# Weight buffers 68 bytes longer, and four raw buffers instead of five, in a one-core transformer layer

## The chip, the core and the metric

The kernel runs on one core of a Trainium2 chip. The core has a matrix engine (TensorE, written PE in the profile; its weight loads are PEld), a vector engine (VectorE, DVE), a scalar engine (ScalarE, ACT), a general engine (GpSimd, POOL) and a sequencer that mostly issues transfers (SyncE, SP). They run their own instruction streams in order and wait for one another by semaphores. Operands lie in an on-chip memory of 128 partitions (SBUF); matrix results go to a second one (PSUM) of eight banks. Transfers between SBUF and the large off-chip memory are carried out by 16 DMA engines.

The metric is the device time of one execution in microseconds (us), lower is better.

## The reference

One decoder layer on 256 tokens of width 2048, all in float32:

- `h = rmsnorm(x)`, then one projection `h @ w_in` into q, k, v of eight attention heads (A) and the low-rank latents of eight more (B);
- A: causal attention in three dilated windows, merged by their softmax denominators; B: latent attention, whose q, k and v come from the latents through `w_uq` and `w_ukv`;
- `x = x + rmsnorm(concat(A, B) @ w_out)`;
- `x = x + rmsnorm(relu(rmsnorm(x) @ w_up)**2 @ w_down)`, where `w_up` is 2048 x 8192 and `w_down` 8192 x 2048.

Nearly all of the arithmetic is in the five matrix products with the large weights; the two of the feed-forward part alone are 134 MB.

## The kernel before

**Split products.** A float32 product is computed as three products of a shorter format. Each operand is split into a part `hi`, rounded to that format, and the rest `lo`; then `a @ w` is `a_hi @ w_hi + a_hi @ w_lo + a_lo @ w_hi`. Each of the three is one matmul on PE with a 128 x 128 block of activations as the operand that is loaded first (PEld) and 512 columns of the weights as the one that streams through (function `three`, and `proj` in the attention part; the helper `mm` is line 296, so nearly every matmul has that line).

**The weight stream.** Class `Weights` takes the weights in the order in which PE will use them, in tiles of 128 partitions x 1024 columns (512 KB). For each tile `emit` does the following, and this is the code that the change touches:

1. `load` takes the next buffer with the tag `raw` and issues the transfer on SP (line 190). There are `RAW_BUFS` such buffers, used in turn; the transfer has to wait until the tile that used the buffer last has been read by its last reader, a subtraction on DVE.
2. ACT rounds `raw` into a buffer `hi` (line 306, or 310 where a gain is multiplied in).
3. DVE subtracts, `lo = raw - hi` (line 307, or 311 with the gain). After that the raw buffer is free.

There are `W_BUFS = 8` buffers for `hi` and as many for `lo`; they come free when PE has used the tile. `emit` runs `W_AHEAD = 6` tiles ahead of the one that PE is about to use. The small pieces of `x` transposed that the first projection needs go through the same raw buffers (`x_load`, line 527).

**Made tiles.** A part of the feed-forward products is computed with seven block products in place of eight (function `seven_products`). For these, DVE first adds blocks of weights that POOL loads in 1 MB pieces (`ab`, `ab_down`, `c` and others, line 374; in the last groups of `w_up` two raw buffers instead), and the sums are split like weights.

**Order.** The whole program order is written by the Python code, which keeps a clock of its own (class `Flow`): chains such as the softmax of a head or the evacuation of an accumulator are started with a delay, and their instructions are put between the matmuls when that clock passes. So every engine's order is fixed; on ACT and DVE the splits of weights that are still far ahead stand in one row with the evacuations that PE waits for soon. An up-projection's evacuation is: `r = relu(acc)` on ACT (line 937), four transposes on PE (`rt`, line 300), a square on ACT (line 949).

**Where the tiles lie.** The left side of SBUF holds first small constants, then the pool `wp` with raw, `hi` and `lo` buffers, then what the current part needs; activations are on the right. In the built program every raw, `hi` and `lo` buffer is 4096 bytes per partition long, and all of them begin at an address that is 480 modulo 512 (the first `hi` at 38880). The same holds for nearly every activation block that PE loads for a split product, which is 128 columns, or 512 bytes, of a tile that begins at 480 modulo 512. Small padding tiles such as `con_pad` and `pa_pad` see to that.

Of the kernel before, what the change touches and what calls it, by code (L numbers as in the profile page):

```python
# [19 lines left out]
F32R = mybir.dt.float32r  # L20
# [6 lines left out]
P = 128  # L27
# [18 lines left out]
CW = 1024  # L46
# [24 lines left out]

RAW_BUFS, W_BUFS, W_AHEAD, AHEAD_NORM = 5, 8, 6, 4

APART = (5, 7)

# [91 lines left out]
class Weights:  # L169
# [23 lines left out]
    def emit(self, upto):  # L193
        upto = min(upto, self.done.index(False) + self.limit, len(self.specs))
        while len(self.tiles) < upto:
            i = len(self.tiles)
            spec = self.specs[i]
            make = len(spec) == 1
            for f in self.first.pop(i, ()):
                f()  # L200
            if not make:
                src, nk, n, g = (*spec, None)[:4]
                w = nk * n
                raw = self.load(src if len(src.shape) == 3 else src.rearrange("(k p) n -> p k n", p=P), w, f"raw{i}")
                for f in self.after.pop(i, ()):
                    f()
            hi = self.pool.tile([P, CW], F32R, tag="hi", bufs=self.bufs, name=f"hi{i}")
            lo = self.pool.tile([P, CW], F32R, tag="lo", bufs=self.bufs, name=f"lo{i}")
            if make:
                spec[0](hi, lo)  # L210
                self.tiles.append((hi, lo))
                continue

            def v(t):
                return t[:, :w].rearrange("p (k n) -> p k n", k=nk)

            cuts = [(o, min(o + 512, w)) for o in range(0, w, 512)] if i < FINE else [(0, w)]
            for o, e in cuts:
                self.split_fn(hi[:, o:e], lo[:, o:e], raw[:, o:e], g)
            self.tiles.append((v(hi), v(lo)))  # L220
# [1088 lines left out]
```

## Time and profile before

| | |
|---|---|
| median of 2 runs | 1047.33 us (1047.23 to 1047.43) |
| profiled execution, first to last instruction (span) | 1045.7 us |
| PE busy in it | 1035.7 us, 99% |
| DVE busy | 838.7 us, 80% |
| ACT busy | 630.4 us, 60% |
| POOL busy | 51.5 us, 5% |
| bytes moved by DMA | 229.33 MB, mean 219 GB/s |

The profile gives one span for the execution and no other time of its own; the runs' median is 1.6 us above it, which is what lies around the first and the last instruction together with the difference from one execution to the next. A busy PE need not be PE at its best pace, since the end of a matmul is modelled; the distance from one matmul's start to the next is the better measure. In the tables of waits, "A <- B" means that engine A stood idle until B's instruction had ended. A row such as "x4 ... 4.62" is four instructions in a row, which took 4.62 us together.

### The profile page before, as it was taken

How to read it: one execution, taken by the hardware profiler on the slowest of the kernel's cores; microseconds unless marked ns; L12 is line 12 of the kernel's file. 1: busy time of each engine (PE TensorE's matmuls, PEld its weight loads, DVE VectorE, ACT ScalarE, POOL GpSimd, SP SyncE). 2: the span in 40 equal slices, each digit the busy share in tenths (PEclk: the TensorE clock that was granted, in tenths of full speed). 3: DMA queues.
4: the chain of work that ended last, by engine and by line, in shares of the span. 5: the costliest groups of instructions: out<-in, count | busy, mean ns of one | idle time of the engine just before them, and what ended most of it. 6: DMA issues, size and time to landing. Idle time of an engine off the chain costs nothing.

```text
span 1045.7 us, 13378 instructions
## 1 busy us (share of the span) xinstructions
PE 1035.7 (99%) x4837; PEld 863.2 (83%) x4837; DVE 838.7 (80%) x1122; ACT 630.4 (60%) x848; POOL 51.5 (5%) x83
## 2 busy tenths in 40 slices
PE   9999999999999999999999999999999999999996
PEld 6888889888888888888888888888888888888885
DVE  6676536567557669999999999897899978999995
ACT  6674436565545566665765667666567564766661
POOL 0000000000000000000000000000000000111100
PEclk9999999999999999999999999999999999999998
DMA  9975547454447295646657356378778767698952
GB/s 303 370 229 148 140 129 241 146 162 153 150 156 236 92 360 188 216 147 207 202 185 246 121 201 207 113 253 325 274 276 303 265 232 261 238 332 323 356 204 83
DMA packets 79938, 229.33 MB, mean 219 GB/s; under 512 B 6912, under 2 KB 11520, under 8 KB 79488
## 3 DMA queue, kind: packets, MB, share of 16 engines
q1 hardware_dynamic: 64576, 171.47, 48.9%
q0 software_dynamic: 14864, 56.63, 15.2%
q8 instruction: 38, 0.62, 0.3%
q10 hardware_dynamic: 432, 0.37, 0.1%
q14 instruction: 28, 0.23, 0.1%
HBM read 212.72 MB, written 15.73 MB: 218 GB/s over the span
## 4 chain that ended last, share of the span: by engine, by line
PE 97%; DVE 1%; issue 1%; ACT 0%; POOL 0%; DVEq 0%; POOLq 0%; ACTq 0%
PE y L296 25%; PE acc_u L296 24%; PE acc_o L296 8%; PE m L296 7%; PE md L296 5%; PE acc_qk L296 4%; PE acc_v L296 4%; PE acc_ckv L296 2%; PE acc_ukv L296 2%; PE acc_q L296 2%; PE acc_cq L296 2%; PE acc_k L296 2%; PE acc_uq L296 2%; PE rt L300 1%; PE sc_b L296 1%
## 5 line engine op out<-in xcount | busy, mean ns | idle before, releaser
L307 DVE TENSOR_TENSOR lo<-raw,hi 128x1024 fp32r<-128x1024 f32 (+3 forms) x213 | 241.5, 1152 | 89.8 <-ACT hi L306 89.1
L306 ACT ACTIVATE hi<-raw 128x1024 fp32r<-128x1024 f32 (+3 forms) x213 | 209.9, 999 | 73.6 <-PE y L296 16.1
L296 PE MATMUL y<-hi,uhi 128*128 128x512 f32 x370 | 144.4, 390 | 0.0
L296 PE MATMUL y<-hi,ulo 128*128 128x512 f32 x370 | 144.1, 389 | 0.0
L296 PE MATMUL y<-lo,uhi 128*128 128x512 f32 x370 | 144.0, 389 | 0.0
L296 PE MATMUL acc_u<-hi,hT_hi 128*128 128x512 f32 x356 | 141.7, 398 | 0.0
L296 PE MATMUL acc_u<-hi,hT_lo 128*128 128x512 f32 x356 | 139.2, 391 | 0.4 <-DVE hT_lo L307 0.4
L296 PE MATMUL acc_u<-lo,hT_hi 128*128 128x512 f32 x356 | 138.9, 390 | 0.0
L311 DVE SCALAR_TENSOR_TENSOR lo<-raw,gcol,hi 128x1024 fp32r<-128x1024 f32 x74 | 92.5, 1279 | 9.5 <-ACT hi L310 9.5
L310 ACT ACTIVATE hi<-raw,gcol 128x1024 fp32r<-128x1024 f32 x74 | 83.7, 1148 | 25.0 <-DMA raw<-in_w_up 11.7
L296 PEld LDWEIGHTS y<-hi,ulo 128*128 128x128 f32 x370 | 69.5, 188 | 14.4
L296 PEld LDWEIGHTS y<-lo,uhi 128*128 128x128 f32 x370 | 69.5, 188 | 14.3
L296 PEld LDWEIGHTS y<-hi,uhi 128*128 128x128 f32 x370 | 69.5, 188 | 14.2
L296 PEld LDWEIGHTS acc_u<-hi,hT_lo 128*128 128x128 f32 x356 | 66.8, 188 | 14.9 <-DVE hT_lo L307 0.8
L296 PEld LDWEIGHTS acc_u<-lo,hT_hi 128*128 128x128 f32 x356 | 67.0, 188 | 12.8
L296 PEld LDWEIGHTS acc_u<-hi,hT_hi 128*128 128x128 f32 x356 | 67.0, 188 | 12.8
L306 ACT ACTIVATE hi<-u 128x1024 fp32r<-128x1024 f32 (+1 forms) x38 | 37.4, 990 | 49.2 <-DVE u L366 35.4
L307 DVE TENSOR_TENSOR lo<-st_down,hi 128x1024 fp32r<-128x1024 f32 x42 | 50.4, 1220 | 3.0 <-ACT hi L306 2.8
L296 PE MATMUL acc_o<-hi,mixT_hi 128*128 128x512 f32 x128 | 51.8, 405 | 0.0
L306 ACT ACTIVATE hi<-st_down 128x1024 fp32r<-128x1024 f32 x42 | 43.9, 1052 | 12.6 <-PE y L296 9.5
L296 PE MATMUL acc_o<-hi,mixT_lo 128*128 128x512 f32 x128 | 50.2, 392 | 0.0
L296 PE MATMUL acc_o<-lo,mixT_hi 128*128 128x512 f32 x128 | 50.0, 391 | 0.0
(328 smaller groups left out, 2087.7 us busy)
## 6 DMA issues: line engine op xcount, KB each, us to landing
raw<-in_w_down SPq DMA_DIRECT2D x86, 512.0 KB, 5.8
raw<-in_w_up SPq DMA_DIRECT2D x76, 512.0 KB, 4.6
raw<-in_w_in SPq DMA_DIRECT2D x55, 512.0 KB, 4.9
ab<-in_w_up POOLq DMA_DIRECT2D x22, 1024.0 KB, 5.4
raw<-in_w_out SPq DMA_DIRECT2D x32, 512.0 KB, 4.2
ab_down<-in_w_down POOLq DMA_DIRECT2D x11, 1024.0 KB, 7.1
ukeep<-ulo SPq DMA_DIRECT2D x15, 512.0 KB, 7.0
ulo<-ukeep POOLq DMA_DIRECT2D x15, 512.0 KB, 6.2
```

The lines of the kernel that those rows point to most:

```text
L296: nc.tensor.matmul(out, a, b, start=start, stop=stop)
L300: nc.tensor.transpose(out, a, ident)
L306: nc.scalar.activation(hi, src, AF.Copy)
L307: nc.vector.tensor_tensor(out=lo, in0=src, in1=hi.bitcast(F32), op=OP.subtract)
L310: nc.scalar.activation(hi, src, AF.Copy, scale=g)
L311: nc.vector.scalar_tensor_tensor(out=lo, in0=src, scalar=g, in1=hi.bitcast(F32), op0=OP.mult, op1=OP.subtract)
```

## The change

Two constants and two lines. Each of the eight `hi` and eight `lo` buffers gets 17 more columns of 4 bytes, 4164 bytes in place of 4096, of which only the first 1024 columns are used, as before. There are four raw buffers where there were five.

```diff
-RAW_BUFS, W_BUFS, W_AHEAD, AHEAD_NORM = 5, 8, 6, 4
+RAW_BUFS, W_BUFS, W_AHEAD, AHEAD_NORM = 4, 8, 6, 4
+
+
+W_PAD = 17
...
-            hi = self.pool.tile([P, CW], F32R, tag="hi", bufs=self.bufs, name=f"hi{i}")
-            lo = self.pool.tile([P, CW], F32R, tag="lo", bufs=self.bufs, name=f"lo{i}")
+            hi = self.pool.tile([P, CW + W_PAD], F32R, tag="hi", bufs=self.bufs, name=f"hi{i}")[:, :CW]
+            lo = self.pool.tile([P, CW + W_PAD], F32R, tag="lo", bufs=self.bufs, name=f"lo{i}")[:, :CW]
```

In the built program a buffer begins at the next multiple of 32, so the distance from one to the next becomes 4192 bytes. The eight `hi` buffers then begin at 480, 64, 160, 256, 352, 448, 32 and 128 modulo 512, and the eight `lo` buffers at 224, 320, 416, 0, 96, 192, 288 and 384: the sixteen multiples of 32, each once. The raw buffers stay at 480. With one raw buffer fewer, what follows on the left side begins 2560 bytes lower, five times 512, so it keeps its address modulo 512; the right side stays where it is.

The instructions of all engines and their order are the same as before, but for line numbers that are 3 higher below the constants. What differs is for what SP's transfers wait. This is the start of SP's row before, with the waits in brackets; `xraw` are the pieces of transposed x, and both kinds take raw buffers in turn:

```order
L527 DMA xraw_102<-in_xt 128x257
L190 DMA raw_104<-in_w_in 128x512
L190 DMA raw_112<-in_w_in 128x512
L527 DMA xraw_129<-in_xt 128x257
L190 DMA raw_133<-in_w_in 128x2x512
L527 DMA xraw_141<-in_xt 128x2x257 [waits DMAHW0_49,DVE_49]
L190 DMA raw_147<-in_w_in 128x2x512 [waits DMAHW1_49,DVE_49]
```

And the same place in the changed program:

```order
L530 DMA xraw_102<-in_xt 128x257
L193 DMA raw_104<-in_w_in 128x512
L193 DMA raw_112<-in_w_in 128x512
L530 DMA xraw_129<-in_xt 128x257
L193 DMA raw_133<-in_w_in 128x2x512 [waits DMAHW0_49,DVE_49]
L530 DMA xraw_141<-in_xt 128x2x257 [waits DMAHW1_49,DVE_49]
L193 DMA raw_147<-in_w_in 128x2x512 [waits DMAHW2_49,DVE_49]
```

No row has changed its place. The first transfer that waits for DVE to free a buffer is now the fifth, `raw_133`, and from there on each transfer waits for the subtraction of the tile four before it, no longer five before it.

## The prediction

> **What bounds the kernel now.** I read the busy times first, then the chain that ended last, then PE's waits, then the spacing of matmuls.
>
> ```profile
> span 1045.7 us, 13378 instructions
> PE 1035.7 (99%) x4837; PEld 863.2 (83%) x4837; DVE 838.7 (80%) x1122; ACT 630.4 (60%) x848; POOL 51.5 (5%) x83
> PE 97%; DVE 1%; issue 1%; ACT 0%; POOL 0%; DVEq 0%; POOLq 0%; ACTq 0%
> PE warm L521 <- DVE zero L518: 1.2, 1, 1.2
> PE acc_u L296 <- DVE hT_lo L307: 0.4, 1, 0.4
> PE qrt L300 <- DVE qT L772: 0.2, 1, 0.2
> ```
>
> PE is the bound from end to end: 97% of the chain is its own work, and the last three rows, all of its waits, come to 1.8 us. So the time can change in two ways only: PE's matmuls follow each other at another pace, or PE begins to wait. The pace is read from runs of matmuls in the chain (start, us, count):
>
> ```profile
> 145.60 2.40 PE acc_ckv L296 x18
> 746.46 16.32 PE y L296 x72
> ```
>
> 72 matmuls of 512 columns in 16.32 us are 226.7 ns each; 18 of 288 columns in 2.40 us are 133.3 ns. The difference, 93.3 ns for 224 columns, is 0.417 ns a column; 512 columns are 213.3 ns, and **13.3 ns are left over** at either size. It is the one thing on PE that an address could be behind.
>
> It is not always so even. In the timeline of PE (start, us, instruction), ten matmuls go by from the first to the second of these rows, 17 from the second to the third:
>
> ```profile
> 499.67 0.40 PE L296 MATMUL acc_u<-lo,hT_hi 128*128 128x512 f32 x1
> 501.97 0.39 PE L296 MATMUL acc_u<-hi,st 128*128 128x512 f32 x1
> 505.82 0.39 PE L296 MATMUL acc_u<-lo,hT_hi 128*128 128x512 f32 x1
> ```
>
> That is 230 ns and then 226.5 ns: behind a group of transposes, at the same addresses, PE is 3.3 ns slower for a while, with no wait to name.
>
> **The raw buffers.** No instruction is added or moved; from the fifth raw transfer on, each is held by a later subtraction. What a buffer's turn takes stands in the DMA issues (KB each, median us from issue to landing) and in the groups of the splits (busy, mean ns):
>
> ```profile
> raw<-in_w_down SPq DMA_DIRECT2D x86, 512.0 KB, 5.8
> raw<-in_w_up SPq DMA_DIRECT2D x76, 512.0 KB, 4.6
> raw<-in_w_in SPq DMA_DIRECT2D x55, 512.0 KB, 4.9
> L307 DVE TENSOR_TENSOR lo<-raw,hi 128x1024 fp32r<-128x1024 f32 (+3 forms) x213 | 241.5, 1152 | 89.8 <-ACT hi L306 89.1
> L306 ACT ACTIVATE hi<-raw 128x1024 fp32r<-128x1024 f32 (+3 forms) x213 | 209.9, 999 | 73.6 <-PE y L296 16.1 <-DMA raw<-in_w_in 14.1 <-PE acc_v L296 10.2
> L310 ACT ACTIVATE hi<-raw,gcol 128x1024 fp32r<-128x1024 f32 x74 | 83.7, 1148 | 25.0 <-DMA raw<-in_w_up 11.7 <-PE acc_u L296 8.2 <-PE acc_o L296 3.1
> ```
>
> Landing, rounding and subtraction of a tile of `w_in` are 4.9 + 1.0 + 1.15 = 7.1 us, of `w_down` 5.8 + 1.0 + 1.15 = 8.0 us; `w_up` lies at 4.6 + 1.15 + its longer subtraction, about 7.0 us. Five buffers give one tile in 1.4 to 1.6 us at best, four in 1.75 to 2.0 us. PE takes 12 matmuls of 226.7 ns for a tile, 2.7 us. **On the mean four are enough**; the cost lies in bursts, where the splits already catch up with the transfers. Those are the waits of ACT for a raw landing, and the hold that SP has on it (total us, times, longest):
>
> ```profile
> ACT hi L306 <- DMA raw<-in_w_in: 14.1, 17, 2.2
> ACT hi L310 <- DMA raw<-in_w_up: 11.7, 7, 5.6
> ACT hi L306 <- DMA raw<-in_w_down: 7.4, 9, 2.0
> SPq L190 <- DVE lo L307: 423.2, 162, 18.9
> SPq L190 <- DVE lo L311: 280.2, 67, 17.2
> ```
>
> SP is nearly always held at a raw transfer by a subtraction, so losing a buffer does delay issues. Behind the held transfer the other transfers of SP queue up (x, the gains, kept u tiles). What waits for the landing is ACT, and behind its rounding stand the evacuations. In such a stretch each tile comes a quarter of a turn less a fifth of it later, 0.05 x 7 to 8 us, or 0.35 to 0.4 us. There are 17 + 7 + 9 = 33 waits: 33 x 0.4 = 13.2 us.
>
> How much of it reaches PE is read at two places. At the start:
>
> ```profile
> 2.59 0.43 SPq L190 DMA_DIRECT2D raw<-in_w_in  x1
> 3.39 0.48 DVE L544 SCALAR_TENSOR_TENSOR xT_lo<-xraw,xT_hi 128x256 fp32r<-128x256 f32 x1
> 7.75 1.15 ACT L306 ACTIVATE hi<-raw 128x512 fp32r<-128x512 f32 x2 [1.08 <-DMA raw<-in_w_in]
> 8.43 0.51 PE L296 MATMUL acc_qk<-hi,xT_hi 128*128 128x512 f32 x1
> ```
>
> The fifth transfer (2.59) will wait for the subtraction that frees the first buffer, which ends at 3.87: 1.3 us later. ACT stood waiting for just this landing, and PE follows ACT by 0.7 us. All of it shows, up to 1.3 us. In the last groups of the up-projection:
>
> ```profile
> 683.99 1.16 ACT L310 ACTIVATE hi<-raw,gcol 128x1024 fp32r<-128x1024 f32 x1 [5.58 <-DMA raw<-in_w_up]
> 697.30 1.06 ACT L306 ACTIVATE hi<-raw 128x1024 fp32r<-128x1024 f32 x1 [1.92 <-DMA raw<-in_w_down]
> 698.68 1.06 ACT L306 ACTIVATE hi<-raw 128x1024 fp32r<-128x1024 f32 x1 [0.32 <-DMA raw<-in_w_down]
> 702.86 0.67 ACT L937 ACTIVATE r<-acc_u,rstd_pre 128x512 f32<-128x512 f32 x1
> 706.32 0.60 PE L300 MATMUL rt<-ident,r 128*128 128x128 f32 x4
> ```
>
> The evacuation `r` at 702.86 stands behind these roundings; it ends at 703.5 and PE transposes it at 706.32, so 2.8 us are in hand, and less than that at most such places. I take this slack off once, since PE that has waited is late for good and gives later chains the same lead as before: 13.2 - 2.3 to 2.8, about **11 us**. If nothing of a landing's delay is hidden and every one of the 33 waits grows by a whole step of DVE, 1.15 us, it is 33 x 1.15 = 38 us, less 2.8, or 35 us. If slack takes all, it is nothing; W_AHEAD alone is 6 x 2.7 = 16 us of weights in hand for PE itself, which is why I expect the loss on the evacuations and not on weights. A gain is excluded here, as no transfer can start earlier. Of the two ends I stay nearer to zero, since most stretches have no wait for a landing at all.
>
> [...]
>
> **The addresses.** No row shows a weight tile at other addresses in a product of 512 columns. The nearest row is `acc_ckv` above: it reads a tile in two cuts of 288 columns, the second 1152 bytes further on, which is 96 modulo 512, with activations still at 480. Its 18 matmuls run at 133.3 ns, with the same 13.3 ns left over as in `y`, where both are at 480. So an offset of 128 bytes costs PE nothing; offsets of 32 and 64 are not shown. The bounds: from below all of 13.3 ns goes, from above PE stays as uneven as in the timeline, 230 ns and single steps of 233. I take **zero**, the value of the nearest row. ACT and DVE write to these buffers too:
>
> ```profile
> 600.00:650.00 50.00, 50.00 (x230) 41.41 (x229) 48.31 (x54) 33.27 (x38) 2.85 (x4) 1.00 0.54 188
> ```
>
> DVE is busy for 48.31 of these 50 us and PE for all 50, with PE at its even pace in most of it; I find no sign that the engines disturb each other. A DVE that lost 4% by the addresses would run out of slack here, from 400 to 650 us; up to some 5 us, inside the range.
>
> The sum: 1045.7 + 11 + 0 = 1056.7 for a profiled execution. The runs' median stands 1.6 us above the span before, so **1058 us**. Noise is small (1047.23 to 1047.43); about 2% of the time, 21 us, is what I count as a difference that a measurement can tell from no change.
>
> **Rivals.**
>
> *The raw cut is hidden.* For it: PE has nearly no waits and six tiles in hand. Against it: ACT's 33 waits, and the start, where 1 us must show. Time: 1047 to 1049. Chance 0.12.
>
> *The addresses slow PE.* The weights no longer lie at the same place modulo 512 as the activation block that is loaded meanwhile. If that keeps PE in the uneven state, each product costs 3.3 ns (230) to 6.3 ns (233) more. Of 512-column products there are some 4,035: 3 x 370 for `y`, 3 x 356 for `acc_u`, 3 x 128 for `acc_o`, the rest in smaller groups. That is 13 to 25 us on top of 1058, or 1071 to 1083, slower than before by over 2%. It decides from about 2.5 ns a matmul, where 10 + 11 us pass 21. Against it: `acc_ckv`, and that the uneven stretches come at 480 as well, behind transposes. Chance 0.18.
>
> *The addresses free PE.* If the 13.3 ns come from both operands beginning at 480, some of the sixteen addresses lose them. [...] Against it: the offset of 128 that changed nothing. Chance 0.10, and 0.04 that it passes the 2%.
>
> [...]
>
> *The change does not do what it says.* It does: the built program has the sixteen addresses, and SP's fifth transfer waits.
>
> **How the numbers follow.** Forecast 0.60 (raw cut shows, addresses do not), its own range 1049 to 1070, with 0.10 above the 2% mark of 1068; hidden 0.12; slowed PE 0.18, of which 0.15 above 1068; freed PE 0.10, of which 0.04 below 1026. Faster 0.04, slower 0.25, within 2% 0.71. The range goes from 1044, which leaves out most of the freed case, to 1082, which is also the 35 us of the uncovered raw cut (1047 + 35).
>
> **What would show it.** In the profile after: the spacing of `y` in its long runs at 226.7 ns (addresses), ACT's waits for raw landings at 45 us or more where they were 33, PE's waits grown by several us in all and their releasers ACT or DVE, not weights; the fifth transfer issued near 3.9 us and the matmul of 8.43 at 9.3 to 9.7; the transposes near 706 late by 8 to 11 us. The prediction is wrong if the spacing is another, or if the late evacuations cost PE less than 5 or more than 20 us.

## The result, and the profile after

The changed kernel takes **1079.20 us** (median of 2 runs, 1078.26 to 1080.14), where the kernel before takes 1047.33. The ratio is 1.0305, with an interval of 1.0275 to 1.0334. Forecast were 1058 us: the sign was right, and the loss, 32 us, is three times the 11 us expected. It lies inside the range of 1044 to 1082, in the case that the prediction held for a rival, "the addresses slow PE".

The profiled execution has a span of 1076.5 us, 30.8 us more than before. The page's busy times and chain of the kernel after:

```profile
span 1076.5 us, 13375 instructions
PE 1058.7 (98%) x4837; PEld 863.9 (80%) x4837; DVE 839.7 (78%) x1122; ACT 630.6 (59%) x848; POOL 50.3 (5%) x83
...
PE 77%; DVE 8%; DMA 8%; ACT 4%; issue 3%; SPq 0%; POOL 0%; DVEq 0%; POOLq 0%; ACTq 0%
```

The page counts three instructions fewer than before; the five engines' counts are the same. PE does the same 4837 matmuls in 1058.7 us where it took 1035.7, and its share of the chain falls from 97% to 77%: for a fifth of the time, what ended last now goes through transfers, roundings and subtractions. So both of the ways the prediction named have been taken, another pace and waits.

The pace first, from the chain (start, us, what, count): the long runs of `y`, and `acc_ckv`.

```profile
770.41 16.72 PE y L299 x72
...
151.01 2.39 PE acc_ckv L299 x18
```

72 matmuls of 512 columns take 16.72 us and no longer 16.32: 232.2 ns each in place of 226.7. The 18 matmuls of 288 columns take 2.39 us, as before (2.40).

Then the waits: those of PE, and those of ACT for a raw landing (total us, times, longest).

```profile
PE rt L303 <- ACT r L940: 5.4, 3, 2.9
PE sc_a L299 <- DVE qkT_a L659: 2.2, 1, 2.2
PE warm L524 <- DVE zero L521: 1.2, 1, 1.2
PE acc_u L299 <- DVE hT_lo L310: 0.4, 1, 0.4
PE acc_u L299 <- DVE c L1046: 0.2, 1, 0.2
```

```profile
ACT hi L313 <- DMA raw<-in_w_up: 25.5, 15, 6.2
ACT hi L309 <- DMA raw<-in_w_in: 24.5, 23, 2.6
ACT hi L309 <- DMA raw<-in_w_down: 20.1, 14, 3.8
```

PE's waits come to 9.4 us, against 1.8 before. ACT's three rows come to 70.1 us in 52 waits, against 33.2 us in 33. The work itself of ACT and DVE on the padded buffers has not changed; from the page's groups (busy, mean ns of one):

```profile
L310 DVE TENSOR_TENSOR lo<-raw,hi 128x1024 fp32r<-128x1024 f32 (+3 forms) x213 | 241.9, 1152 | 108.7 <-ACT hi L309 107.6
L309 ACT ACTIVATE hi<-raw 128x1024 fp32r<-128x1024 f32 (+3 forms) x213 | 210.2, 999 | 103.1 <-DMA raw<-in_w_in 24.5
```

1152 ns and 999 ns, as before. These two engines show no cost of the addresses.

One wait shows how the two meet. The timeline of ACT, behind the up-projection, in the kernel after:

```profile
728.76 1.06 ACT L309 ACTIVATE hi<-raw 128x1024 fp32r<-128x1024 f32 x1 [3.83 <-DMA raw<-in_w_down]
729.72 0.67 ACT L940 ACTIVATE r<-acc_u,rstd_pre 128x512 f32<-128x512 f32 x1
```

The evacuation `r` stands behind a rounding that waited 3.83 us for its landing, as the prediction had it, and PE's transposes `rt` wait 2.9 us for `r`. What PE does behind that wait was in no step of the prediction. The stretches of 1 or 2 us from the same trace (us, PE busy and count, PEld, DVE, ACT, POOL, PEclk, DMA share, GB/s):

```profile
728.00:730.00 2.00, 0.00 (x0) 0.00 (x0) 0.60 (x2) 1.24 (x2) 0.00 (x0) 1.00 0.99 371
...
731.00:732.00 1.00, 1.00 (x5) 0.90 (x4) 0.22 (x2) 1.00 (x2) 0.00 (x0) 0.50 1.03 422
...
734.00:735.00 1.00, 1.00 (x8) 0.87 (x7) 0.00 (x0) 1.00 (x1) 0.00 (x0) 1.00 1.02 397
```

The granted clock (the number behind POOL's) is **0.50** for some three microseconds after the wait, and 1.00 again from 734 on. The whole stretch of 730 to 734 has a mean clock of 0.57, so this one wait cost up to 0.43 x 4 = 1.7 us beside its own 2.9; the last 0.3 us of the wait itself lie in the slow stretch.

The first matmul of each stage in the two traces shows where the 30.8 us come from. Two columns for kernels of the experiments stand beside (us behind the kernel before, at the stage's first matmul):

| stage, and its start before | after | four raw buffers alone | addresses alone |
|---|---|---|---|
| values of A, 49.6 | 1.3 | 2.9 | 1.4 |
| latents of B, 145.4 | 5.4 | 7.0 | 3.0 |
| output projection, 253.1 | 5.8 | 7.0 | 3.5 |
| up-projection, 354.1 | 7.3 | 7.0 | 5.0 |
| down-projection (`y`), 701.6 | 18.5 | 15.7 | 12.2 |
| `md`, 741.5 | 23.8 | 20.9 | 13.0 |
| end of the products, 1037.1 | 30.8 | 20.9 | 20.1 |

The raw buffers cost at the beginning, bit by bit in the groups of the up-projection, and behind the change to the down-projection, and nothing from `md` on; the addresses cost all along.

### The profile page after: what moved, and what is told of

Read it like the earlier page. It is cut to its first block, busy times and chain, and to the rows that moved or that the text cites. A ratio compares the mean times of both kernels' runs of the same rounds, so it can differ in the third digit from the quotient of the medians.

```text
span 1076.5 us, 13375 instructions
## 1 busy us (share of the span) xinstructions
PE 1058.7 (98%) x4837; PEld 863.9 (80%) x4837; DVE 839.7 (78%) x1122; ACT 630.6 (59%) x848; POOL 50.3 (5%) x83
## 4 chain that ended last, share of the span: by engine, by line
PE 77%; DVE 8%; DMA 8%; ACT 4%; issue 3%; SPq 0%; POOL 0%; DVEq 0%; POOLq 0%; ACTq 0%
PE y L299 25%; PE acc_u L299 15%; PE acc_o L299 8%; PE md L299 5%; PE m L299 5%; DMA raw<-in_w_in 4%; DMA raw<-in_w_up 3%; DVE lo L310 3%; PE acc_ckv L299 2%; PE acc_ukv L299 2%; PE acc_cq L299 2%; PE acc_v L299 2%; PE acc_k L299 2%; DVE lo L314 2%; ACT hi L309 2%
## 5 line engine op out<-in xcount | busy, mean ns | idle before, releaser
L310 DVE TENSOR_TENSOR lo<-raw,hi 128x1024 fp32r<-128x1024 f32 (+3 forms) x213 | 241.9, 1152 | 108.7 <-ACT hi L309 107.6
L299 PE MATMUL y<-lo,uhi 128*128 128x512 f32 x370 | 146.8, 397 | 0.0
L313 ACT ACTIVATE hi<-raw,gcol 128x1024 fp32r<-128x1024 f32 x74 | 84.6, 1152 | 41.6 <-DMA raw<-in_w_up 25.5
```

Of the source, the lines that this page charges most:

```text
L299: nc.tensor.matmul(out, a, b, start=start, stop=stop)
L310: nc.vector.tensor_tensor(out=lo, in0=src, in1=hi.bitcast(F32), op=OP.subtract)
L313: nc.scalar.activation(hi, src, AF.Copy, scale=g)
```

## The experiments

The expectations name theories by letters. A is that the change has two causes, buffers and addresses, with a price each; B is that there is only one. C, O and V are three forms of an address effect: C, that the address 480 is special; O, that it is the offset between the weights that stream and the activation block that is loaded; V, that it is the change of address from one matmul to the next. Ratios are given where a kernel was timed in several rounds; the other kernels were run once, beside the kernel before at 1047.3 to 1047.8 us.

**Each half alone.** First four raw buffers with the old addresses:

```diff
-RAW_BUFS, W_BUFS, W_AHEAD, AHEAD_NORM = 5, 8, 6, 4
+RAW_BUFS, W_BUFS, W_AHEAD, AHEAD_NORM = 4, 8, 6, 4
```

> Four raw buffers, no padding. Theory A (two causes: the raw cut by waits, the addresses by PE's spacing): 1055 to 1060 us, spacing of y in its long runs 226.7 ns as before, ACT waits for raw landings of 65 to 75 us as in the changed kernel. Theory B (one cause: with raw buffers short, PE is disturbed and stays at an uneven pace of 232 ns): 1075 to 1080 us, spacing 232 ns.

Measured: 1068.73 us (1065.32 to 1069.97), ratio 1.0196 (1.0171 to 1.0222), span 1066.6. Pace, waits of PE, waits of ACT:

```profile
767.37 16.32 PE y L296 x72
```

```profile
PE rt L300 <- ACT r L937: 8.8, 7, 3.4
...
PE acc_qk L296 <- ACT hi L306: 2.3, 3, 1.2
PE sc_a L296 <- DVE qkT_a L656: 2.3, 1, 2.3
```

```profile
ACT hi L306 <- DMA raw<-in_w_in: 24.2, 20, 2.8
ACT hi L306 <- DMA raw<-in_w_down: 23.0, 16, 3.8
ACT hi L310 <- DMA raw<-in_w_up: 22.1, 12, 6.3
```

The pace is untouched, 226.7 ns. The waits of ACT grow by 36 us, from 33.2 to 69.3, and those of PE by 14.6, from 1.8 to 16.4 (five smaller rows are not shown). The time itself lies above the 1055 to 1060 us that A expected and below the 1075 of B; the pace and ACT's waits are those of A. Behind the two longest, the clock falls; in the stretches around the wait of `sc_a` (same columns as above):

```profile
81.00:83.00 2.00, 0.00 (x0) 0.00 (x0) 1.82 (x2) 0.55 (x2) 0.00 (x0) 1.00 1.00 359
83.00:87.00 4.00, 3.90 (x11) 3.29 (x12) 3.33 (x8) 3.52 (x6) 0.00 (x0) 0.57 0.84 264
87.00:91.00 4.00, 4.00 (x20) 3.32 (x20) 2.30 (x7) 3.11 (x8) 0.00 (x0) 1.00 0.71 219
```

That is 1.7 us, and as much after the wait of 3.4 us at 725. 14.6 + 3.4 are 18.0 of the 20.9 us; the remaining 2.9 are not separated. Some of them may be the first products behind a wait: behind the one that ends at 9.16 us in this trace, the next four start 0.34, 0.23, 0.29 and 0.23 us apart.

Then the addresses alone, with five raw buffers. To make room, an output of the last squares, which nothing reads, was put into an unused part of another tile; the pad is 32 bytes, which gives the same sixteen addresses:

```diff
-hi = self.pool.tile([P, CW], F32R, tag="hi", ...)
-lo = self.pool.tile([P, CW], F32R, tag="lo", ...)
+hi = self.pool.tile([P, CW + 8], F32R, tag="hi", ...)[:, :CW]
+lo = self.pool.tile([P, CW + 8], F32R, tag="lo", ...)[:, :CW]
...
-junk = dpl["dp"].tile([P, 512], BF16, tag="junk", ...)
+junk = late["st"][:, 2 * CW + 512:2 * CW + 768].bitcast(BF16)
```

> Five raw buffers, hi and lo buffers 32 bytes longer (again sixteen addresses modulo 512, in other order); to make room, the output of the last squares that nobody reads goes into an unused part of another tile. Theory A: 1067 to 1071 us, spacing 231 to 233 ns, ACT waits for raw landings near 33 us. Theory B: 1047 to 1049 us, spacing 226.7 ns.

Measured: 1067.34 us (1066.65 to 1067.62), ratio 1.0188 (1.0172 to 1.0204), span 1065.8. Pace and waits of PE:

```profile
759.61 16.71 PE y L296 x72
```

```profile
PE warm L521 <- DVE zero L518: 1.2, 1, 1.2
PE acc_u L296 <- DVE hT_lo L307: 0.4, 1, 0.4
PE acc_qk L296 <- ACT hi L306: 0.4, 2, 0.2
```

PE waits for 2.0 us, as it did before, and a product of 512 columns takes 232.1 ns on the mean of the long runs. **A holds and B falls**: each half costs 20 to 21 us when it is alone. Together they cost 32 and not 41. What fits is that a slower PE leaves ACT and DVE more time between two evacuations: in the changed kernel its waits are 9.4 us, with four buffers at the old pace 16.4, and one stretch at half clock follows in place of two. No run tests this by itself.

**What about an address is slow.** Four raw buffers as in the first run, and all weight buffers moved by 256 bytes, to 224 modulo 512:

```diff
-RAW_BUFS, W_BUFS, W_AHEAD, AHEAD_NORM = 5, 8, 6, 4
+RAW_BUFS, W_BUFS, W_AHEAD, AHEAD_NORM = 4, 8, 6, 4
...
+wp.tile([P, 64], F32, name="w_shift")
...
+wp.tile([P, 64], F32, name="w_shift_back")
```

> Four raw buffers, all hi and lo buffers at one address modulo 512, but 224 in place of 480; all else at 480. Theory A, in the form that weights and activations have to agree modulo 512: 1076 to 1081 us, spacing 231 to 233 ns. If an even multiple of 128 does no harm (as in acc_ckv): 1055 to 1060 us and 226.7 ns. If it is the change of address from one matmul to the next that costs: 226.7 ns, since here there is none.

Measured: 1069.15 us, span 1067.4:

```profile
768.17 16.32 PE y L296 x72
```

Then weights and activations all at 0 modulo 512, by other sizes of three padding tiles, again with four raw buffers:

```diff
-con.tile([P, 32], F32, name="con_pad")
+con.tile([P, 40], F32, name="con_pad")
...
-mix.tile([P, 64], F32, name="mix_pad")
+mix.tile([P, 184], F32, name="mix_pad")
...
+late["up"].tile([P, 120], F32, name="up_pad")
```

> Four raw buffers; weights and all activations that PE loads for split products moved together from 480 to 0 modulo 512. Theory A: 1055 to 1060 us, spacing 226.7 ns, since they agree. Theory C (480 itself is the good address): 1076 to 1081 us, 231 to 233 ns.

Measured: 1070.30 us, span 1068.5:

```profile
769.04 16.32 PE y L296 x72
```

Both are the first run again, with its pace of 226.7 ns; the second lies 0.3 us above that run's highest time. So 480 as such makes no difference here, and C falls. The next two kernels have five raw buffers; these and all that follow with other addresses have the moved output too, which by itself costs nothing (the identity's run below has it, at a ratio of 1.0001). In one, the weights are moved by 32 bytes, all to 0, while the activations stay at 480:

```diff
+wp.tile([P, 8], F32, name="w_shift")
...
+wp.tile([P, 120], F32, name="w_shift_back")
```

> Five raw buffers; all hi and lo buffers at 0 modulo 512, activations left at 480 (an offset of 32). The output of the last squares goes into an unused part of another tile, as in e2. Theory O (what counts is the offset between weights and activations; 0, 128 and 256 are harmless, smaller steps not): 1067 to 1071 us, spacing of y 231 to 233 ns. Theory V (what counts is that the address changes from one matmul to the next): 1047 to 1049 us, 226.7 ns.

Measured: 1071.59 us, span 1069.8, 24.1 us more than before; in the chain:

```profile
762.00 16.80 PE y L296 x72
...
149.58 2.40 PE acc_ckv L296 x18
```

233.3 ns, though all weights lie at one address modulo 512. The raw buffers stayed at 480 here, so the weights' distance to them has changed too. The end of the down-projection, where hardly a transfer is under way any more, tells the two apart (columns as above, and PE's last row in the chain):

```profile
1050.00:1060.00 10.00, 10.00 (x44) 8.07 (x43) 4.71 (x10) 2.06 (x6) 0.56 (x1) 1.00 0.08 26
```

```profile
1050.40 5.61 PE y L1190 x24
```

The DMA engines are busy for 8% of it and move 26 GB/s, which is half of a 512 KB tile in the ten microseconds, and PE still takes 233.8 ns for each of its last 24 products; the same 24 take 5.46 us, 227.5 ns each, in the kernel before. So the loss is there with hardly a transfer beside it.

In the other, `hi` stays at 480 and only `lo` moves by 256 bytes, so that the address changes from matmul to matmul:

```diff
+if not i:
+    self.pool.tile([P, 64], F32, name="lo_shift")
...
+wp.tile([P, 64], F32, name="lo_shift_back")
```

> Five raw buffers; all hi buffers at 480 as before, all lo buffers at 224 modulo 512, so the address changes by 256 with nearly every matmul. Theory O: 1047 to 1049 us, 226.7 ns, since an offset of 256 is harmless. Theory V: 1067 to 1071 us, 231 to 233 ns.

Measured: 1048.47 us, span 1046.7:

```profile
747.45 16.32 PE y L298 x72
```

226.7 ns. So a change of address by 256 bytes from matmul to matmul costs nothing here, and a constant offset of 32 bytes costs 6.6 ns a product: **O holds, V falls**. A kernel in which `hi` and `lo` of a tile share their address modulo 512 and only the tiles differ (480, 0, 32, ... 192) agrees:

```diff
+hi = self.pool.tile([P, CW + 8], F32R, tag="hi", ...)[:, :CW]
+if not i:
+    self.pool.tile([P, 64], F32, name="lo_shift")
+lo = self.pool.tile([P, CW + 8], F32R, tag="lo", ...)[:, :CW]
...
+wp.tile([P, 64], F32, name="lo_shift_back")
```

> Five raw buffers; hi and lo of a tile begin at the same address modulo 512, but each of the eight pairs at another (480, 0, 32, 64, 96, 128, 160, 192). Theory O: 1062 to 1068 us, 230 to 232 ns, since six of eight pairs have a harmful offset. Theory V: the address changes with every sixth or twelfth matmul only: 1049 to 1060 us, 227 to 230 ns.

Measured: 1067.13 us, span 1065.4, `y` at 16.71 us for 72, the same as with sixteen addresses. The two kernels differ in that all `lo` lie 256 bytes apart, and the 44 rows of `y` among the longest pieces of their chains agree in count and to within 0.01 us: four of 72 at 16.71 us in both, those of 24 at 5.54 to 5.60 us. So 256 bytes more or less made no difference here, at an offset of 0 or over the sixteen addresses.

**How the price goes with the offset.** The kernel with 32 bytes again, with 64 and with 128:

```diff
+wp.tile([P, 16], F32, name="w_shift")
...
+wp.tile([P, 112], F32, name="w_shift_back")
```

> Five raw buffers; all hi and lo at 32 modulo 512, activations at 480: an offset of 64. The output of the last squares goes into an unused part of another tile. If harmless offsets are the multiples of 64: 1047 to 1049 us, spacing 226.7 ns. If they are the multiples of 128: 1067 to 1072 us, 231 to 234 ns.

Measured: 1055.07 us, between the two cases that were expected, span 1053.3:

```profile
751.25 16.48 PE y L296 x72
```

```diff
+wp.tile([P, 32], F32, name="w_shift")
...
+wp.tile([P, 96], F32, name="w_shift_back")
```

> The same with an offset of 128 (hi and lo at 96 modulo 512). If multiples of 128 are harmless, as acc_ckv seemed to say: 1047 to 1049 us, 226.7 ns. If only 0 and 256 are: 1067 to 1072 us, 231 to 234 ns, and acc_ckv's even pace belongs to its shorter matmuls.

Measured: 1067.72 us, span 1065.9:

```profile
759.39 16.74 PE y L296 x72
...
148.18 2.40 PE acc_ckv L296 x18
```

So products of 512 columns take 226.7 ns at offsets of 0 and 256 bytes, 233.3 at 32, 228.9 at 64 and 232.5 at 128. The last row is the one that matters for the prediction: in the same trace, with the offset that costs `y` 5.8 ns, the products of 288 columns still take 133.3 ns. **They show next to nothing of the effect**: at 32, 64 and 128 bytes their long rows stay within 1.1 ns of those before. A third size was in the traces as well, the products `acc_uq` of 384 columns. The first row is from the kernel before, the second from the one with 32 bytes:

```profile
214.63 2.11 PE acc_uq L296 x12
219.30 2.12 PE acc_uq L296 x12
```

They do not show it either. It is the products of 512 columns that lose.

**The uneven steps behind transposes.** In the kernel before, PE follows at 230 ns for a while after a group of transposes. The identity matrix that they read begins at 384 modulo 512; here it was moved to 480:

```diff
+con.tile([P, 24], F32, name="ident_pad")
 ident = con.tile(...)
+con.tile([P, 104], F32, name="ident_back")
```

> Five raw buffers, weights at 480 as before; the identity that the transposes stream moves from 384 to 480 modulo 512, so it agrees with the r that is loaded against it. If the uneven stretches behind transposes are the same effect: fewer steps above 229 ns, 1043 to 1046 us. If they are merely what any interruption leaves: 1047 to 1048 us.

Measured: 1047.92 us (1047.43 to 1048.61), ratio 1.0001 (0.9992 to 1.0011). Its address is not the cause, and there is nothing to gain there.

**How many raw buffers.** First seven, with seven pairs of `hi` and `lo` to make room:

```diff
-RAW_BUFS, W_BUFS, W_AHEAD, AHEAD_NORM = 5, 8, 6, 4
+RAW_BUFS, W_BUFS, W_AHEAD, AHEAD_NORM = 7, 7, 6, 4
```

> Seven raw buffers and seven pairs of hi and lo, no padding; the same memory as before. If raw buffers are still short with five (33 us of ACT waits for landings before): 1042 to 1046 us, those waits below 20 us. If five are enough and the eighth pair matters more: 1048 to 1056 us, with waits of ACT for PE to free pairs.

Measured: 1051.41 us (1051.26 to 1052.25), ratio 1.0036 (1.0022 to 1.0051). Two of ACT's waits:

```profile
ACT hi L306 <- PE y L296: 73.4, 70, 6.8
ACT hi L306 <- DMA raw<-in_w_in: 13.8, 20, 1.8
```

The wait for landings of `w_in` is what it was with five (14.1 us), that of `w_up` falls from 11.7 to 3.4 us and that of `w_down` is gone, but ACT waits longer for PE to free a pair, 73.4 us where it was 54.2. More than five raw buffers are worth less than the eighth pair. Then three, with all eight pairs:

```diff
-RAW_BUFS, W_BUFS, W_AHEAD, AHEAD_NORM = 5, 8, 6, 4
+RAW_BUFS, W_BUFS, W_AHEAD, AHEAD_NORM = 3, 8, 6, 4
```

> Three raw buffers, no padding. A buffer's turn of 7.1 to 8.0 us over three is 2.4 to 2.7 us a tile, which reaches PE's 2.7 us: no longer bursts alone but the mean is short. If the landing's delay is the mechanism: 1100 to 1130 us, with PE's waits at the same places and more (start, first heads, evacuations), and ACT waiting over 130 us for raw landings. If the cost came from elsewhere and grew evenly with each buffer: about 1087 us.

Measured: 1109.66 us, span 1107.9, mean clock 0.989 where it was 0.997. ACT's waits and the pace:

```profile
ACT hi L306 <- DMA raw<-in_w_down: 64.7, 38, 4.4
ACT hi L310 <- DMA raw<-in_w_up: 62.9, 32, 7.6
ACT hi L306 <- DMA raw<-in_w_in: 45.9, 30, 3.0
```

```profile
802.12 16.32 PE y L296 x72
```

From five to four buffers the loss is 21 us, from four to three another 41. With three, a tile comes every 2.4 to 2.7 us by the turns of 7.1 to 8.0 us in the prediction, and PE needs one every 2.7 us, so next to nothing can be caught up; still the long runs of `y` keep 226.7 ns. The lower clock alone is 0.008 x 1108, some 9 us of it. In these kernels a buffer less costs waits, and the even pace is 226.7 ns with five, four and three.

None of these kernels is faster than the one before.

## Why the prediction was wrong

**What bounds the kernel.** Right. PE is the bound, and time went the two ways that were named; the third, a lower clock after a wait, was not seen. The profile before has no wait of PE over 1.2 us; its mean clock of 0.997 comes from its end, where the clock is 0.50 from 1040.3 us on, behind the last product of 1037.5. That was the only place where this could be read.

**The addresses: "I take zero, the value of the nearest row".** This is the step that failed. The row was `acc_ckv`, whose second cut lies 128 bytes off and runs at the even pace. The reading of that row was right; carrying it over to products of 512 columns was not. At the same offset these lose 5.8 ns, and the row of 288 columns stays between 132 and 134 ns in every kernel here. A row that cannot show an effect is no evidence against it. The step looked for one leftover, 13.3 ns at either size, and took it for the place where any effect of an address would appear; the effect came on top of it, at 512 columns and not at 288 or 384.

What happened is the rival "the addresses slow PE", by its own sum: 3.3 to 6.3 ns for 4,035 products, 13 to 25 us; measured are 5.4 ns in the long runs and 20.1 us. (The trace has 4,083 such products, one per cent more.) Its condition, an offset between the streaming weights and the block that is loaded, is what the shifted kernels show: 233.3, 228.9 and 232.5 ns at 32, 64 and 128 bytes where 0 and 256 have 226.7. What in PE costs the time is not shown; as nearly all blocks begin at one address modulo 512, whether it is the block in use or the one loaded meanwhile is not told apart. That the total of 1079 also fell into the rival's 1071 to 1083 is in part luck: its raw term, 11 us, was half of what four buffers cost alone, and that the two losses overlap made up for it. It was given 0.18, mostly because of that one row. The uneven steps behind transposes, counted against it as well, are a separate matter. For the other rival, "the addresses free PE", no run shows a gain: no row of `y` above is under 226.7 ns a product.

**The raw cut: 33 x 0.4 us, less 2.3 to 2.8 us of slack, about 11 us.** The mechanism was right, the size was not: alone it costs 20.9 us of span. Of the places, the start and the evacuations of the up-projection were named; the first scores `sc_a`, with 2.3 us of wait and 1.7 us of clock, were not. Three terms were off. First, the waits of ACT for landings grew by 36 us and not by 13.2, both longer and more (48 for 33); that is nearly the upper bound of the prediction, a whole step of DVE for each wait. Second, slack took more than was granted: PE's waits grew by 14.6 of the 36 us, so some 21 were hidden, not 2.5. These two errors nearly cancel, 14.6 against 11, which is luck. Third, each of PE's two longest waits was followed by a stretch at a clock of 0.50, 3.4 us together, and 2.9 us more are not separated. The prediction had no term for these.

In the changed kernel itself this part is smaller: 7.6 us of waits more than before and up to 1.7 us of clock. The other 21.5 of the 30.8 us are left for the pace, 5.3 ns for each product of 512 columns, where the long runs of `y` show 5.5.

**On the mean four are enough, the cost lies in bursts.** Right: with four buffers, nothing more is lost from `md` to the end.

**The start.** Half right. The fifth transfer was to go out near 3.9 us and the matmul of 8.43 to come at 9.3 to 9.7. The rows of the kernel after, by SP's and ACT's timelines:

```profile
3.77 0.38 SPq L193 DMA_DIRECT2D raw<-in_w_in  x1
...
7.52 1.15 ACT L309 ACTIVATE hi<-raw 128x512 fp32r<-128x512 f32 x2 [1.61 <-DMA raw<-in_w_in]
```

It went out 1.2 us later and yet was rounded 0.2 us earlier than before, and the matmul came at 8.42. In the run with four buffers alone, the same transfer went out at 3.86 and the matmul came at 9.16. So "all of it shows" took the landing time as given. Issued later, the transfer landed 3.7 us after its issue in the one execution and 4.6 in the other, where it had been 5.1; why is not shown.

**The late evacuations.** The transposes of 706.32 were to be late by 8 to 11 us. They are 18.6 us late after the change and 15.7 with four buffers alone. Of the two signs of being wrong that the prediction names, the first is there: the spacing is another. The second is not: the late evacuations `rt` made PE wait for 5.4 us, within the 5 to 20.

**The sum of the two.** For the rival the losses were to be added, "13 to 25 us on top of 1058". They overlap: 21 and 20 us give 32.

## What to carry to other kernels

In a kernel like this one, try the streamed operand of a 512-column product at the address of the activation blocks that PE loads, or 256 bytes from it (226.7 ns a product here, against 228.9 to 233.3 at 32, 64 and 128 bytes), and test a layout on products of the size that carries the time, since smaller ones may not show the effect: those of 288 columns took 132 to 134 ns at every offset. Count staging buffers by the bursts: a buffer less costs what the engines behind it cannot hide (21 us from five to four here, 41 from four to three), and a clock of 0.50 behind a wait of PE can come on top, here up to 1.7 us behind waits of 2.9, 2.3 and 3.4 us. When two costs feed on the same slack, expect less than their sum; here 31 us of 41.

## What the hardware showed that was not expected

**An offset of 32, 64 or 128 bytes slowed products of 512 columns here, and not those of 288 or 384.** Those of 288 took 132 to 134 ns and those of 384 columns 173 to 177 ns at every offset. For 512 columns: 226.7 ns at an offset of 0 or 256 bytes, 233.3 at 32, 228.9 at 64, 232.5 at 128, 232.1 over sixteen addresses; the offsets counted are those of the weights against the activation block, modulo 512, and with both at 0 or both at 480 there is no loss. Why it depends on the length, and why 64 costs less than 32 or 128, stays open, as do the 13.3 ns that are left over at the even pace.

**The clock fell to half behind some waits of PE, and not by their length alone.** In the changed kernel the wait of 2.9 us is followed by a clock of 0.50, while the wait of 2.2 us before `sc_a` is followed by 1.00. With four raw buffers the wait of 2.3 us at the same place is followed by half clock (0.57 in the stretch of 83 to 87 above), and with three one of 2.0 us for the roundings of `acc_qk` is, behind 8 us. In the changed kernel's trace the half clock lasts 3.41 us, from 730.15 to 733.56, and comes again at 1071.48, behind the last product; from the first change to the last are 341.33 us, which is 100 times 3.413. Stretches of that length, laid so that the changes fall on their borders, show this (columns as above; the first four are from the changed kernel, the last two from the one with three raw buffers):

```profile
78.20:81.61 3.41, 1.64 (x10) 1.15 (x8) 2.07 (x3) 1.16 (x2) 0.00 (x0) 1.00 0.91 303
81.61:85.03 3.42, 3.02 (x15) 2.60 (x16) 2.65 (x8) 3.10 (x3) 0.00 (x0) 1.00 0.94 323
...
726.74:730.15 3.41, 0.84 (x4) 0.37 (x2) 2.01 (x3) 1.39 (x2) 0.00 (x0) 1.00 0.98 342
730.15:733.56 3.41, 3.12 (x10) 2.64 (x11) 2.15 (x2) 3.31 (x6) 0.00 (x0) 0.50 1.03 420
...
8.16:11.57 3.41, 1.54 (x6) 1.00 (x7) 1.56 (x3) 1.95 (x4) 0.00 (x0) 1.00 0.81 274
11.57:14.98 3.41, 3.41 (x9) 2.66 (x9) 1.82 (x4) 1.15 (x2) 0.00 (x0) 0.50 0.73 225
```

PE was idle for 1.77 us of the first stretch, and the next one has the full clock; it was idle for 2.57 and 1.87 us of the third and the fifth, and half clock follows. Divided in this way from end to end, the changed kernel's trace has no other stretch with more than 1.6 us idle up to its last product. The stretch with the last product, 1068.07 to 1071.48, is idle for 3.1 us, and 0.50 follows; in the kernel before, the 3.41 us up to 1040.34 are idle for 2.8 us, and 0.50 follows there too. The wait of 2.2 us before `sc_a` lies across the border at 81.61, with 1.8 us on the one side and 0.4 on the other; the wait of 2.3 us in the run with four buffers, 80.80 to 83.10, ends just where its half clock begins. That the idle time within such a stretch decides is the author's reading of these rows, and no run was made to test it. By that reading it is partly chance whether a wait of some 2 us costs this.
